# Low parts of the mixed and normed inputs all on VectorE, first products of the mixing all on ScalarE

## Chip, cores and metric

The kernel runs on one core of a Trainium2 chip. The metric is the device time of one execution in microseconds (us). The engines are TensorE (PE; its weight loads are PEld), VectorE (DVE), ScalarE (ACT), GpSimd (POOL) and SyncE (SP). Each takes its own instructions in order; they wait for each other by semaphores.

## What is computed

The model is a trunk of two layers, each followed by a SwiGLU FFN, on 1024 tokens of width 1024 in float32. The first layer mixes by chunked gating and by pooling, the second is RWKV-7 time mixing with a recurrence over the tokens. The change touches how the inputs of the RWKV-7 layer are made:

```python
def rwkv7_time_mix(h, mu, w_r, w_k, w_v, ...):
    xx = jnp.pad(h, ((0, 0), (1, 0), (0, 0)))[:, :-1] - h
    xr, xw, xk, xv, xa, xg = [h + xx * mu[i] for i in range(6)]
    r = xr @ w_r
    wlog = -jax.nn.softplus(-(w0 + jnp.tanh(xw @ w1) @ w2)) - 0.5
    k = xk @ w_k
    v = xv @ w_v
    a = jax.nn.sigmoid(a0 + (xa @ a1) @ a2)
    g = jax.nn.sigmoid(xg @ g1) @ g2
    ...
    y = wkv7_scan(rh, decay, kh, vh, -kk, kk * ah)
    ...
    return (y * g) @ w_o

def swiglu(hn, w_gate, w_up, w_down):
    return (jax.nn.silu(hn @ w_gate) * (hn @ w_up)) @ w_down
```

Here `h` is the normed input of the layer. A mixed input such as `xg` is, for every channel, `h[t] * (1 - mu) + h[t-1] * mu`.

## The kernel before

Tokens are worked in two halves of 512, channels in eight tiles of 128 (`KT` = 8). A float32 operand of a matmul is split into a high part that PE takes in its fast float32 format and a low part, the rest; a product is then three matmuls (`mm3`, L344 to L346: high by high, high by low, low by high). The split of a tile is a copy to the high part on ACT (L145) and a subtraction for the low part (L146), on DVE unless another engine is named. Weights come by DMA from ACT's queue (L115) into a ring of three `raw` tiles and are split in the same way into `whi` and `wlo`; some small weights go through `stack` (L151 on ACT, L153 on DVE), among them `w2` and `a2`, shown as `w` and `a` in the profile.

The order of the program: the first layer for both halves, then for each half the projections and the recurrence of the RWKV-7 layer, with parts of the FFNs of either half worked beside them so that PE has dense work. `beside` (L694) runs such a part of an FFN (and for the second half the output projection of the first) and, between its matmuls, the steps of `side` (in `project_gate`): the split of the normed input in eight steps (`split_steps`, 128 x 513 a tile, one token more than a half), then `mix_steps` for the inputs of `g`, `r` and `k`. That is one stage for each half. `project` then makes `k`, `r` and the decay for one pair of heads after another, mixes the input of `v` by a fourth call of `mix_steps`, and multiplies it. `recur` (the recurrence) comes next, again with FFN work beside it.

`mix_steps` makes for each of the eight tiles: a first product `mix = hn * (1 - mu)` (L882 on DVE or L886 on ACT, by the table `MIX_ENG`: even tiles ACT, odd tiles DVE), a second product with a sum (L887 on DVE, the shifted input times `mu`, added in place), a high part on ACT (L891) and a low part (L875, by the table `LOW_ENG`: even tiles DVE, odd tiles POOL). The low part of a tile is written in the code after the high part of the next one. The `mix` tiles have two buffers, so the first product of a tile waits until the low part of the tile two before it has been made. For `g`, `k` and `v` the parts are called `xhi` and `xlo`, for `r` and for the normed input `ahi` and `alo`.

Other work on POOL near the change: the scaling after a sigmoid (`sigm`, L775), the square root by a power (`rsqrt`, L349; in `project` on `rn`, the norms of the keys, which PE then spreads by L1037), `kkn` (L1051), and the clearing of tiles for the inversion (L1111).

Instructions are not issued in the order of the code: a scheduler with a timeline model of the engines sets the order on each of them, so that an edit in one place can move instructions elsewhere.

Of the kernel before, what the change touches and what calls it, by code (L numbers as in the profile page):

```python
# [9 lines left out]
F32 = mybir.dt.float32  # L10
F32R = mybir.dt.float32r
AF = mybir.ActivationFunctionType
ALU = mybir.AluOpType
# [9 lines left out]
GN_EPS = 64e-5  # L23
DEC = math.exp(-0.5)
WINS = (2, 4, 8, 16)

MIX_ENG, LOW_ENG = "adadadad", "dpdpdpdp"


RATIO, AHEAD, INV, FINE = 3.0, 450, 5, 1  # L30
# [8 lines left out]
def tile_trunk(  # L39
# [8 lines left out]
    act, dve, pool, pe, sp = nc.scalar, nc.vector, nc.gpsimd, nc.tensor, nc.sync  # L48
    x = x.flatten_outer_dims()
    out = out.flatten_outer_dims()  # L50
# [43 lines left out]
    omv = const.tile([P, P], F32, name="omv")  # L94

    def col(c):
        return vec[:, c : c + 1]
# [35 lines left out]
    def take(key):  # L133
        i = pos[0]
        assert plan[i][0] == key, (plan[i][0], key)
        pos[0] += 1
        split_at(i)
        load_at(i + 1)
        if i + 1 in raws:
            load_at(i + 2)  # L140
        split_at(i + 1)
        return ready.pop(i)

    def split(src, hi, lo, eng=None):
        act.activation(hi, src, AF.Copy)  # L145
        (eng or dve).tensor_tensor(out=lo, in0=src, in1=hi.bitcast(F32), op=ALU.subtract)  # L146

    def stack(los):

        def go(n, src, dst, _):  # L150
            act.activation(dst, src, AF.Copy)  # L151
            r = los[n]
            dve.tensor_tensor(out=dst[r], in0=src[r], in1=dst[r].bitcast(F32), op=ALU.subtract)  # L153

        return go
# [19 lines left out]
    def v3(t):  # L175
        return t.rearrange("p (k m) -> p k m", m=P)
# [79 lines left out]
    def groups_of(first):  # L256

        rest = list(range(first, 18))
        return [[f, f + 1] for f in range(0, first, 2)], [rest[i : i + 3] for i in range(0, len(rest), 3)], [18, 19], [20, 21]

    n0, n1, a, b = groups_of(BESIDE[0])
    G0B = n0, n1 + [a], [b]
    n0, n1, a, b = groups_of(BESIDE[1])
# [65 lines left out]
    def mmt():  # L329
        return pst("mm")  # L330
# [12 lines left out]
    def mm3(o, whi, wlo, xhi, xlo, first, last):  # L343
        pe.matmul(o, whi, xhi, start=first, stop=False)  # L344
        pe.matmul(o, whi, xlo, start=False, stop=False)  # L345
        pe.matmul(o, wlo, xhi, start=False, stop=last)  # L346
# [37 lines left out]
    def act_tiles(pool_, n=HT):  # L384
        return [pool_.tile([P, KT, n], F32R, tag=t, name=t) for t in ("ahi", "alo")]
# [113 lines left out]
    for h in range(2):  # L499
        ops = [mmt() for _ in range(4)]  # L500
        for kp in range(4):
# [4 lines left out]
            for kk in range(2):  # L506
                k = 2 * kp + kk
# [11 lines left out]
    for tt in range(8):  # L519
        dve.tensor_scalar(  # L520
            out=vt[tt], in0=vt[tt], scalar1=vss[:, tt : tt + 1], scalar2=None, op0=ALU.mult
# [46 lines left out]
    for m in ORD_Z:  # L568
# [4 lines left out]
        for h in range(2):  # L573
# [22 lines left out]
            if h == 0:  # L596
                dve.scalar_tensor_tensor(
                    out=s[:, 16 : 16 + win - 1], in0=s[:, 16 : 16 + win - 1], scalar=float(win),
                    in1=tcnt[:, 0 : win - 1], op0=ALU.mult, op1=ALU.mult,
                )  # L600
            dve.scalar_tensor_tensor(
                out=zq, in0=s[:, 16:], scalar=1.0 / win, in1=zp[:, 16:], op0=ALU.mult, op1=ALU.subtract,
# [13 lines left out]
    for h in range(2):  # L616
        hi, lo = act_tiles((xlp, actp)[h])
# [148 lines left out]
    def dense2(o, whi, wlo, xs, n=P, between=()):  # L766

        wh, wl = v3(whi), v3(wlo)
        for k in range(KT):
            if k < len(between):  # L770
                between[k]()
            mm3(o, wh[:, k, :n], wl[:, k, :n], xs[k][0], xs[k][1], k == 0, k == KT - 1)

    def sigm(dst, th):
        pool.tensor_scalar(out=dst, in0=th, scalar1=0.5, scalar2=0.5, op0=ALU.mult, op1=ALU.add)  # L775
# [14 lines left out]
    def project_norm(h, np_):  # L790

        hn1 = np_.tile([P, KT, 1 + HT], F32, name="hn1")
        if h == 0:
            pool.memset(hn1[:, :, 0:1], 0.0)
        else:
            pool.tensor_copy(hn1[:, :, 0:1], hlast)
        b = norm_scale(h)
        for k in range(KT):
            dve.scalar_tensor_tensor(
                out=hn1[:, k, 1:], in0=H[h][:, k, :], scalar=col(C_MIX + 8 + k), in1=b, op0=ALU.mult, op1=ALU.mult  # L800
            )
        if h == 0:
            pool.tensor_copy(hlast, hn1[:, :, HT : HT + 1])
        return hn1

    def project_gate(h, hn1, kp, xlp, ring):

        xlow = act_tiles(xlp, 1 + HT)
        keep = {}

        def tile_of(tag):
            keep[tag] = kp.tile([P, HT], F32R, tag=tag, name=tag)
            return keep[tag]

        def split_steps():
            for k in range(KT):  # L820
                split(hn1[:, k, :], xlow[0][:, k, :], xlow[1][:, k, :], pool if k % 2 else dve)
                yield

        def lowrank():

            ws = [take(("wa1", h, n)) for n in range(2)]
            o = mmt()
            for k in range(KT):
                for n, (wh, wl) in enumerate(ws):
                    sl = slice(1 - n, 1 - n + HT)  # L830
                    xh, xl = (x[:, k, sl] for x in xlow)
                    mm3(o, v3(wh)[:, k, :], v3(wl)[:, k, :], xh, xl, k == 0 and n == 0, k == KT - 1 and n == 1)
            t = nt.tile([P, HT], F32, tag="nsq", bufs=2, name="low")
            act.activation(t[0:64], o[0:64], AF.Tanh)
            act.activation(t[64:128], o[64:128], AF.Copy)
            lo = tile_of("twlo")
            for n, tag in enumerate(("tw", "ta")):
                hi = tile_of(tag)
                for r in rows:
                    act.activation(hi[r], t[rows[n]], AF.Copy)  # L840
                r = rows[n]
                dve.tensor_tensor(out=lo[r], in0=t[r], in1=hi[r].bitcast(F32), op=ALU.subtract)

        xs = []

        def gate():
            for nm, n in (("g1", P), ("g1b", 96)):
                wg = take((nm, h))
                o = mmt()
                dense2(o[:n], *wg, xs, n)  # L850
                t = nt.tile([P, HT], F32, tag="nsq", bufs=2, name="gt")
                act.activation(t[:n], o[:n], AF.Tanh, scale=0.5)
                sigm(t[:n], t[:n])
                if n == P:
                    split(t, tile_of("ghi"), tile_of("glo"))
                else:
                    stack([slice(64, 96)])(0, t[:n], tile_of("gst")[:n], None)

        def side():
            yield from split_steps()  # L860
            yield from mix_steps(hn1, 5, xs, ring_tiles(ring), kp)
            xr = [x.rearrange("p k t -> p (k t)")[:, : KT * HT].rearrange("p (k t) -> p k t", t=HT) for x in act_tiles(xlp, 1 + HT)]
            yield from mix_steps(hn1, 0, keep["xr"], lambda k: [x[:, k, :] for x in xr], kp)
            yield from mix_steps(hn1, 2, keep["xk"], ring_tiles(ring), kp)

        keep["xr"], keep["xk"] = [], []
        return (side(), lowrank, gate), keep

    def ring_tiles(ring):
        return lambda k: [ring.tile([P, HT], F32R, tag=tag, bufs=8, name=tag) for tag in ("xhi", "xlo")]  # L870

    def mix_steps(hn1, i, res, tiles, kp):

        def low(k, t, hi, lo):
            (pool if LOW_ENG[k] == "p" else dve).tensor_tensor(out=lo, in0=t, in1=hi.bitcast(F32), op=ALU.subtract)  # L875

        prev = None
        for k in range(KT):
            c = C_MU + 8 * i + k
            t = kp.tile([P, HT], F32, tag="mix", bufs=2, name="mix")  # L880
            if MIX_ENG[k] != "a":
                (dve if MIX_ENG[k] == "d" else pool).tensor_scalar(  # L882
                    out=t, in0=hn1[:, k, 1:], scalar1=omv[:, c : c + 1], scalar2=None, op0=ALU.mult
                )
            else:
                act.activation(t, hn1[:, k, 1:], AF.Identity, scale=omv[:, c : c + 1])  # L886
            dve.scalar_tensor_tensor(  # L887
                out=t, in0=hn1[:, k, 0:HT], scalar=col(c), in1=t, op0=ALU.mult, op1=ALU.add
            )
            hi, lo = tiles(k)  # L890
            act.activation(hi, t, AF.Copy)  # L891
            if prev is not None:
                low(*prev)
            prev = k, t, hi, lo
            if k == KT - 1:
                low(*prev)
            res.append((hi, lo))
            yield
# [236 lines left out]
    for b in range(2):  # L1135
        for c0, cmp in ((0, ALU.is_gt), (64, ALU.is_ge)):
            v = gm[rows[b], c0 : c0 + 64]
            pool.affine_select(
                out=v, in_=v, pattern=[[1, 64]], compare_op=cmp, fill=0.0, base=0, channel_multiplier=-1
# [354 lines left out]
    hn1 = project_norm(0, np_)  # L1494
# [43 lines left out]
    hn1 = project_norm(1, np_)  # L1538
# [85 lines left out]
```

## Time and profile before

| | us |
|---|---|
| median of three runs | 2528.8 |
| lowest and highest | 2524.71 and 2532.28 |
| the profiled execution, its own time | 2522.66 |
| its span in the profile | 2520.9 |

The span runs from the first to the last instruction of the profiled execution. The mean clock that PE was granted in it is 0.983 of full speed. How PE's pace, the waits and the other engines look in the stages of the mixing is read in the prediction. Rows of a group read as: line, engine, operation, output and inputs, shapes, count, then busy us and mean ns of one, then the idle time ahead of them and what ended it. Rows of a timeline begin with the start and the duration in us.

The 40 slices of the page (63 us each) show where the stages lie; POOL is busiest where inputs are mixed, in the slices 11 to 14 and 23 to 26:

```
DVE  5445634444865873555457855964654445434443
ACT  6233322222544432333234643433333224323223
POOL 0200000000323410111001222401211000100001
```

### The profile page before, as it was taken

The numbers are of one execution on the slowest core, as the hardware profiler recorded it, in microseconds if no ns is written. First come the engines' busy times: TensorE is split into PE (matmuls) and PEld (weight loads), VectorE is DVE, ScalarE is ACT, GpSimd is POOL, SyncE is SP. The second block draws the span as 40 slices with busy tenths as digits, with TensorE's granted clock in tenths as the row PEclk, the third lists the DMA queues.
The fourth block names the chain that finished last, engine by engine and source line by source line (L and its number), as shares of the span: only waits on it lengthen the run. The fifth ranks groups of instructions, "written<-read, shape, count | busy, mean of one in ns | idle before, by whom it ended". The sixth has DMA issues, their size and how long they took to land.

```text
span 2520.9 us, 37945 instructions
## 1 busy us (share of the span) xinstructions
PE 2432.2 (96%) x15735; PEld 1983.2 (79%) x15735; DVE 1401.8 (56%) x2118; ACT 890.7 (35%) x1335; POOL 299.8 (12%) x298
## 2 busy tenths in 40 slices
PE   8999999999989998999999989899999999999998
PEld 6888888888767786788877667787888878888887
DVE  5445634444865873555457855964654445434443
ACT  6233322222544432333234643433333224323223
POOL 0200000000323410111001222401211000100001
PEclk9999999999999998999999999999999999999999
DMA  5113433323255478433334355585653332423331
GB/s 175 48 59 92 142 109 116 101 92 112 88 156 134 123 204 203 136 113 102 112 118 138 111 179 133 132 230 159 167 150 110 100 107 77 150 88 119 94 92 59
DMA packets 434956, 310.69 MB, mean 123 GB/s; under 512 B 93216, under 2 KB 395424, under 8 KB 433760
## 3 DMA queue, kind: packets, MB, share of 16 engines
q10 hardware_dynamic: 297280, 210.53, 27.9%
q1 hardware_dynamic: 137504, 97.75, 13.7%
q8 instruction: 123, 2.02, 0.3%
q14 instruction: 49, 0.40, 0.0%
HBM read 254.68 MB, written 53.54 MB: 122 GB/s over the span
## 4 chain that ended last, share of the span: by engine, by line
PE 74%; DVE 13%; DMA 7%; issue 3%; ACT 2%; POOL 1%; SPq 0%; ACTq 0%; DVEq 0%; POOLq 0%
PE mm L344 21%; PE mm L345 21%; PE mm L346 20%; PE sm L1168 4%; DVE wlo L146 2%; DMA raw<-in_ffn_w_up_dram 2%; DVE it L1117 1%; DVE mix L887 1%; DVE xi L1122 1%; DMA iat<-at_d 1%; PE yp L1168 1%; DMA raw<-in_ffn_w_down_dram 1%; PE mm L510 1%; PE mm L511 1%; ACT whi L145 1%
## 5 line engine op out<-in xcount | busy, mean ns | idle before, releaser
L344 PE MATMUL mm<-ahi,whi 128*128 128x512 f32 x1952 | 766.9, 394 | 5.1 <-DVE h L423 4.0
L345 PE MATMUL mm<-alo,whi 128*128 128x512 f32 x1952 | 769.1, 394 | 1.6 <-DVE alo L146 1.6
L346 PE MATMUL mm<-ahi,wlo 128*128 128x512 f32 x1952 | 766.5, 393 | 2.6 <-DVE wlo L146 2.6
L145 ACT ACTIVATE whi<-raw 128x1024 fp32r<-128x1024 f32 x288 | 304.3, 1058 | 768.1 <-PE mm L345 608.5
L146 DVE TENSOR_TENSOR wlo<-raw,whi 128x1024 fp32r<-128x1024 f32 x288 | 362.0, 1257 | 309.8 <-ACT whi L145 301.5
L344 PEld LDWEIGHTS mm<-ahi,whi 128*128 128x128 f32 x1952 | 367.9, 189 | 87.2 <-issue 4.5
L346 PEld LDWEIGHTS mm<-ahi,wlo 128*128 128x128 f32 x1952 | 368.2, 189 | 82.3 <-DVE wlo L146 3.4
L345 PEld LDWEIGHTS mm<-alo,whi 128*128 128x128 f32 x1952 | 368.2, 189 | 82.1 <-issue 3.7
L345 PE MATMUL mm<-hidlo,wdhi 128*128 128x512 f32 x624 | 246.6, 395 | 1.3 <-DVE hidlo L672 1.2
L344 PE MATMUL mm<-hidhi,wdhi 128*128 128x512 f32 x624 | 239.8, 394 | 6.6 <-ACT hidhi L671 5.2
L346 PE MATMUL mm<-hidhi,wdlo 128*128 128x512 f32 x624 | 245.5, 393 | 0.0
L423 DVE TENSOR_TENSOR h<-h,mm 128x512 f32<-128x512 f32 x192 | 129.2, 684 | 149.9 <-PE mm L346 149.1
L145 ACT ACTIVATE wdhi<-raw 128x1024 fp32r<-128x1024 f32 x82 | 86.6, 1059 | 254.9 <-DMA raw<-in_ffn_w_down_dram 150.8
L146 DVE TENSOR_TENSOR wdlo<-raw,wdhi 128x1024 fp32r<-128x1024 f32 x82 | 100.4, 1225 | 111.3 <-ACT wdhi L145 105.5
L668 DVE TENSOR_TENSOR sg<-sg,mm 128x512 f32<-128x512 f32 x88 | 60.2, 685 | 165.3 <-PE mm L346 164.9
L344 PEld LDWEIGHTS mm<-hidhi,wdhi 128*128 128x128 f32 x624 | 117.2, 188 | 35.2 <-ACT hidhi L671 7.4
L345 PEld LDWEIGHTS mm<-hidlo,wdhi 128*128 128x128 f32 x624 | 118.2, 189 | 27.9 <-DVE hidlo L672 3.2
L346 PEld LDWEIGHTS mm<-hidhi,wdlo 128*128 128x128 f32 x624 | 118.2, 189 | 24.6 <-issue 0.2
L423 DVE TENSOR_TENSOR hA<-hA,mm 128x512 f32<-128x512 f32 x72 | 48.7, 685 | 77.0 <-PE mm L346 77.0
L349 POOL TENSOR_TENSOR nrs<-nrs,small 128x4 f32<-128x4 f32 x8 | 10.0, 1246 | 625.4 <-DVE nrs L371 625.4
L344 PE MATMUL mm<-xhi,whi 128*128 128x512 f32 (+1 forms) x160 | 66.0, 412 | 4.2 <-ACT k L925 4.2
L672 DVE TENSOR_TENSOR hidlo<-sg,hidhi 128x512 fp32r<-128x512 f32 x88 | 64.5, 733 | 3.8 <-ACT hidhi L671 3.7
(300 smaller groups left out, 2952.1 us busy)
## 6 DMA issues: line engine op xcount, KB each, us to landing
raw<-in_ffn_w_gate_dram ACTq DMA_DIRECT2D x88, 512.0 KB
raw<-in_ffn_w_up_dram ACTq DMA_DIRECT2D x88, 512.0 KB
raw<-in_ffn_w_down_dram ACTq DMA_DIRECT2D x88, 512.0 KB
raw<-in_ab_w_in_dram ACTq DMA_DIRECT2D x16, 512.0 KB
raw<-in_ab_w_out_dram ACTq DMA_DIRECT2D x16, 512.0 KB
raw<-in_rwkv_w_k_dram ACTq DMA_DIRECT2D x16, 512.0 KB
raw<-in_rwkv_w_r_dram ACTq DMA_DIRECT2D x16, 512.0 KB
ar_d<-ar SPq DMA_DIRECT2D x16, 512.0 KB
```

Source lines behind the costliest of these rows:

```text
L145: act.activation(hi, src, AF.Copy)
L146: (eng or dve).tensor_tensor(out=lo, in0=src, in1=hi.bitcast(F32), op=ALU.subtract)
L344: pe.matmul(o, whi, xhi, start=first, stop=False)
L345: pe.matmul(o, whi, xlo, start=False, stop=False)
L346: pe.matmul(o, wlo, xhi, start=False, stop=last)
L423: dve.tensor_tensor(out=H[h][:, m, :], in0=H[h][:, m, :], in1=o, op=ALU.add)
L510: pe.matmul(ops[j], xhi[:, k, sl], whi[:, kk], start=(k == 0), stop=False)
L511: pe.matmul(ops[j], xhi[:, k, sl], wlo[:, kk], start=False, stop=False)
L668: dve.tensor_tensor(out=s, in0=s, in1=o, op=ALU.mult)
L672: dve.tensor_tensor(out=lo, in0=s, in1=hi.bitcast(F32), op=ALU.subtract)
L887: dve.scalar_tensor_tensor(out=t, in0=hn1[:, k, 0:HT], scalar=col(c), in1=t, op0=ALU.mult, op1=ALU.add)
L1168: i = f(*args, **kw)
```

## The change

```diff
--- before.py
+++ after.py
@@ -23,8 +23,6 @@
 GN_EPS = 64e-5
 DEC = math.exp(-0.5)
 WINS = (2, 4, 8, 16)
-
-MIX_ENG, LOW_ENG = "adadadad", "dpdpdpdp"
 
 
 RATIO, AHEAD, INV, FINE = 3.0, 450, 5, 1
@@ -818,7 +816,7 @@
 
         def split_steps():
             for k in range(KT):
-                split(hn1[:, k, :], xlow[0][:, k, :], xlow[1][:, k, :], pool if k % 2 else dve)
+                split(hn1[:, k, :], xlow[0][:, k, :], xlow[1][:, k, :])
                 yield
 
         def lowrank():
@@ -872,18 +870,13 @@
     def mix_steps(hn1, i, res, tiles, kp):
 
         def low(k, t, hi, lo):
-            (pool if LOW_ENG[k] == "p" else dve).tensor_tensor(out=lo, in0=t, in1=hi.bitcast(F32), op=ALU.subtract)
+            dve.tensor_tensor(out=lo, in0=t, in1=hi.bitcast(F32), op=ALU.subtract)
 
         prev = None
         for k in range(KT):
             c = C_MU + 8 * i + k
             t = kp.tile([P, HT], F32, tag="mix", bufs=2, name="mix")
-            if MIX_ENG[k] != "a":
-                (dve if MIX_ENG[k] == "d" else pool).tensor_scalar(
-                    out=t, in0=hn1[:, k, 1:], scalar1=omv[:, c : c + 1], scalar2=None, op0=ALU.mult
-                )
-            else:
-                act.activation(t, hn1[:, k, 1:], AF.Identity, scale=omv[:, c : c + 1])
+            act.activation(t, hn1[:, k, 1:], AF.Identity, scale=omv[:, c : c + 1])
             dve.scalar_tensor_tensor(
                 out=t, in0=hn1[:, k, 0:HT], scalar=col(c), in1=t, op0=ALU.mult, op1=ALU.add
             )
```

`mix_steps` is called eight times and makes 64 mixed tiles. For the 32 odd ones the first product moves from DVE to ACT and the low part from POOL to DVE. The split of the normed input makes 16 tiles, of which eight low parts move from POOL to DVE. Nothing else in the code is changed; lines after the table move up by two, those after the loop of `mix_steps` by seven, so L887, L891 and L875 of before are L880, L884 and L873 of the change.

How the order on the engines comes out is shown at three places. The first is on DVE, in the mixing of the input of `g` for the first half; the numbers in the names tell the tiles apart (`mix_4559` is the third of the eight, `mix_4569` the fourth). Before:

```order
L882 TENSOR_SCALAR mix_4569<-hn1_4353,omv_74 128x512
L887 SCALAR_TENSOR_TENSOR mix_4559<-hn1_4353,vec_73,mix_4559 128x512
L887 SCALAR_TENSOR_TENSOR mix_4569<-hn1_4353,vec_73,mix_4569 128x512
L875 TENSOR_TENSOR xlo_4563<-mix_4559,xhi_4562 128x512
L887 SCALAR_TENSOR_TENSOR mix_4579<-hn1_4353,vec_73,mix_4579 128x512
L882 TENSOR_SCALAR mix_4589<-hn1_4353,omv_74 128x512
L887 SCALAR_TENSOR_TENSOR mix_4589<-hn1_4353,vec_73,mix_4589 128x512
L875 TENSOR_TENSOR xlo_4583<-mix_4579,xhi_4582 128x512
```

The same four tiles on DVE in the change:

```order
L880 SCALAR_TENSOR_TENSOR mix_4559<-hn1_4353,vec_73,mix_4559 128x512
L880 SCALAR_TENSOR_TENSOR mix_4569<-hn1_4353,vec_73,mix_4569 128x512
L873 TENSOR_TENSOR xlo_4563<-mix_4559,xhi_4562 128x512
L873 TENSOR_TENSOR xlo_4573<-mix_4569,xhi_4572 128x512
L880 SCALAR_TENSOR_TENSOR mix_4579<-hn1_4353,vec_73,mix_4579 128x512
L880 SCALAR_TENSOR_TENSOR mix_4589<-hn1_4353,vec_73,mix_4589 128x512
L873 TENSOR_TENSOR xlo_4583<-mix_4579,xhi_4582 128x512
L873 TENSOR_TENSOR xlo_4593<-mix_4589,xhi_4592 128x512
```

The two first products are gone and two low parts have come, and the tiles go in pairs; ahead of the second pair of sums stand on ACT the first products of `mix_4579` and `mix_4589`.

The second place is on DVE at the end of the same stage, where PE needs the weight `w2` for the first pair of heads in `project`; `mix_6561` and `mix_6567` are the first two tiles of the input of `v`. Before:

```order
L153 TENSOR_TENSOR whi_5189<-raw_5090,whi_5189 32x1024
L887 SCALAR_TENSOR_TENSOR mix_6561<-hn1_4353,vec_73,mix_6561 128x512
L882 TENSOR_SCALAR mix_6567<-hn1_4353,omv_74 128x512
L887 SCALAR_TENSOR_TENSOR mix_6567<-hn1_4353,vec_73,mix_6567 128x512
L153 TENSOR_TENSOR w2_5184<-raw_5186,w2_5184 64x1024
L153 TENSOR_TENSOR a2_5185<-raw_5192,a2_5185 64x1024
```

In the change:

```order
L151 TENSOR_TENSOR whi_5189<-raw_5090,whi_5189 32x1024
L873 TENSOR_TENSOR xlo_5014<-mix_5010,xhi_5013 128x512
L873 TENSOR_TENSOR xlo_5021<-mix_5017,xhi_5020 128x512
L880 SCALAR_TENSOR_TENSOR mix_6561<-hn1_4353,vec_73,mix_6561 128x512
L151 TENSOR_TENSOR w2_5184<-raw_5186,w2_5184 64x1024
L151 TENSOR_TENSOR a2_5185<-raw_5192,a2_5185 64x1024
L880 SCALAR_TENSOR_TENSOR mix_6567<-hn1_4353,vec_73,mix_6567 128x512
```

Between the splits of `whi` and `w2` stand now two low parts of the input of `k` and one sum, where two sums and a product stood; the second sum comes behind both splits.

The third place is on POOL in the last pairs of heads of the first half, where the input of `v` is mixed. Before:

```order
L349 TENSOR_TENSOR rn_6283<-rn_6283,small_70 128x8
L875 TENSOR_TENSOR xlo_6571<-mix_6567,xhi_6570 128x512
L1048 TENSOR_SCALAR ar_6342<-kkn_6344 128x8
L875 TENSOR_TENSOR xlo_6585<-mix_6581,xhi_6584 128x512
L1051 TENSOR_TENSOR kkn_6344<-kkn_6344,av_6263 128x512
L775 TENSOR_SCALAR sg_6438<-sg_6438 128x512
L775 TENSOR_SCALAR av_6439<-av_6439 128x512
L875 TENSOR_TENSOR xlo_6599<-mix_6595,xhi_6598 128x512
L1017 COPY pct_1943<-epx_6448 128x8
L349 TENSOR_TENSOR rn_6459<-rn_6459,small_70 128x8
```

In the change:

```order
L347 TENSOR_TENSOR rn_6283<-rn_6283,small_70 128x8
L1041 TENSOR_SCALAR ar_6342<-kkn_6344 128x8
L1044 TENSOR_TENSOR kkn_6344<-kkn_6344,av_6263 128x512
L773 TENSOR_SCALAR sg_6438<-sg_6438 128x512
L773 TENSOR_SCALAR av_6439<-av_6439 128x512
L1010 COPY pct_1943<-epx_6448 128x8
L347 TENSOR_TENSOR rn_6459<-rn_6459,small_70 128x8
```

The low parts are gone from between the steps of the projection; the rest stands in the same order.

## The prediction

> **What bounds the kernel now.** The page comes first. TensorE (PE) is busy for 96% of the span and holds 74% of the chain that ended last; VectorE (DVE) holds 13%, ScalarE (ACT) 2% and GpSimd (POOL) 1%.
>
> ```profile
> PE 2432.2 (96%) x15735; PEld 1983.2 (79%) x15735; DVE 1401.8 (56%) x2118; ACT 890.7 (35%) x1335; POOL 299.8 (12%) x298
> PE 74%; DVE 13%; DMA 7%; issue 3%; ACT 2%; POOL 1%; SPq 0%; ACTq 0%; DVEq 0%; POOLq 0%
> ```
>
> A change that touches no matmul can therefore only win or lose idle time of PE, and only in the stages where it acts. There are four: the two stages in which the mixing runs beside dense work (once for each half of the tokens), and the two in which the v products are mixed. The busy times of PE, PE's loads, DVE, ACT and POOL in them, then PE's clock:
>
> ```profile
> 637.00:727.00 90.00, 78.30 (x334) 61.42 (x332) 84.91 (x106) 54.38 (x82) 30.08 (x26) 0.98 0.34 105
> 1357.00:1467.00 110.00, 96.27 (x400) 73.48 (x399) 98.70 (x129) 62.38 (x95) 33.70 (x26) 0.98 0.41 132
> 855.00:890.00 35.00, 32.00 (x184) 24.98 (x184) 32.62 (x53) 16.68 (x25) 18.70 (x13) 0.85 0.52 137
> 1598.00:1631.00 33.00, 26.45 (x199) 20.61 (x197) 31.11 (x48) 14.90 (x22) 17.53 (x13) 1.00 0.48 134
> ```
>
> DVE is the fullest engine in all four (84.91 of 90 us, 94%, in the first), while PE is idle for 11.7 us of the first and 13.7 us of the second. In these stages DVE sets the pace, although over the whole span it is busy 56%. The waits of PE say the same (us in total, times, longest). Around the first mixing stage:
>
> ```profile
> PE aux L999 <- DVE w L153: 4.6, 1, 4.6
> PE mm L344 <- ACT whi L145: 2.3, 1, 2.3
> PE mm L923 <- DVE whi L153: 2.1, 1, 2.1
> PE mm L344 <- DVE sg L668: 1.5, 1, 1.5
> ```
>
> Around the second:
>
> ```profile
> PE mm L344 <- DVE h L423: 4.0, 1, 4.0
> PE mm L346 <- DVE wlo L146: 2.6, 2, 2.1
> PE aux L999 <- DVE w L153: 1.9, 1, 1.9
> PE mm L345 <- DVE hidlo L672: 1.8, 1, 1.8
> ```
>
> And around each v mixing, the same row in both:
>
> ```profile
> PE aux L1037 <- POOL rn L349: 2.6, 1, 2.6
> ```
>
> Of the first group 8.2 us end on DVE (4.6 + 2.1 + 1.5) and 2.3 us on ACT; the four rows of the second make 10.3 us.
>
> **The change part by part.** Each of the 64 mixed tiles has a first product, a second product with the sum (L887), a high part on ACT (L891) and a low part (L875). For the odd tiles the product leaves DVE (L882) for ACT (L886), and the low part leaves POOL for DVE. Eight lows of the normed input leave POOL too. Durations (min/median/max, ns):
>
> ```profile
> L882 DVE TENSOR_SCALAR mix<-hn,omv x32: 469/475/1907, 643.0 to 1618.1; 128x512 f32<-128x512 f32 x32
> L886 ACT ACTIVATE mix<-hn,omv x32: 706/720/727, 639.1 to 1616.8; 128x512 f32<-128x512 f32 x32
> L875 POOL TENSOR_TENSOR xlo<-mix,xhi x24: 1273/1648/2742, 651.3 to 1626.4; 128x512 fp32r<-128x512 f32 x24
> L875 DVE TENSOR_TENSOR xlo<-mix,xhi x24: 677/678/919, 653.6 to 1628.7; 128x512 fp32r<-128x512 f32 x24
> L887 DVE SCALAR_TENSOR_TENSOR mix<-hn,vec,mix x64: 736/741/1835, 644.7 to 1622.6; 128x512 f32<-128x512 f32 x64
> L146 DVE TENSOR_TENSOR wlo<-raw,whi x288: 951/1225/2356, 13.5 to 2471.9; 128x1024 fp32r<-128x1024 f32 x143, 128x768 fp32r<-128x768 f32 x1
> ```
>
> *Work moved, one mixing stage beside dense work.* Three input sets of eight tiles: DVE loses 12 products, 12 x 0.475 = 5.7 us, and gains 12 lows, 12 x 0.678 = 8.1 us, and 4 lows of the normed input, 4 x 0.68 = 2.7 us. Counted by work alone DVE gets **5.1 us more** on the fullest engine. ACT gets 12 x 0.720 = 8.6 us, which takes it from 54.4 to 63 of 90 us.
>
> *The stretch that goes.* Against that stands what POOL's instructions do to DVE's. The same timeline on POOL, DVE and ACT, where POOL works on one low:
>
> ```profile
> 676.79 3.55 POOL L875 TENSOR_TENSOR alo<-mix,ahi 128x512 fp32r<-128x512 f32 x1 [5.00 <-issue]
> 679.11 1.52 DVE L882 TENSOR_SCALAR mix<-hn,omv 128x512 f32<-128x512 f32 x1
> 680.38 0.72 ACT L886 ACTIVATE mix<-hn,omv 128x512 f32<-128x512 f32 x1 [3.72 <-POOL alo L875]
> 681.13 0.75 DVE L887 SCALAR_TENSOR_TENSOR mix<-hn,vec,mix 128x512 f32<-128x512 f32 x1 [0.51 <-ACT mix L886]
> ```
>
> The product that takes 0.475 us alone takes 1.52 us and ends just after POOL does; POOL's own low takes 3.55 us where its shortest takes 1.27; and ACT stood 3.72 us before the next product, because the tile's buffer was free only when POOL was done, after which DVE stood 0.51 us. The groups of DVE in the first stage show how often that happens:
>
> ```profile
> L887 DVE SCALAR_TENSOR_TENSOR mix<-hn,vec,mix 128x512 f32<-128x512 f32 x26 | 23.5, 916 | 2.6 <-ACT mix L886 2.5
> L146 DVE TENSOR_TENSOR wlo<-raw,whi 128x1024 fp32r<-128x1024 f32 x11 | 15.7, 1432 | 0.3 <-ACT whi L145 0.3
> L882 DVE TENSOR_SCALAR mix<-hn,omv 128x512 f32<-128x512 f32 x13 | 9.3, 718 | 0.0
> L875 DVE TENSOR_TENSOR alo<-mix,ahi 128x512 fp32r<-128x512 f32 x4 | 4.9, 1228 | 0.0
> L1111 POOL MEMSET xi<- 128x2048 f32 x1 | 1.8, 1799 | 0.0
> ```
>
> Means above the medians: 26 x (916 - 741) = 4.6 us, 11 x (1432 - 1225) = 2.3, 13 x (718 - 475) = 3.2, 4 x (1228 - 678) = 2.2; together 12.3 us. The last row is POOL work at the stage's end that stays; a DVE instruction that meets it loses up to its 1.8 us, of which I leave 1.5, so **10.8 us go** with the change.
>
> The Trainium skill, SBUF — State Buffer, section "Who interferes with whom", says that GpSimd and a DVE instruction with two SBUF inputs (or in a two-port mode) lock the same port pair for a whole instruction and that the later one blocks. The direction agrees with the four rows; by the full lock 16 lows at the 1.27 us of the shortest could cost up to 20 us a stage, an estimate, where the groups show 10.8: often POOL is the one held up (its 3.55 us), and no engine needed that result soon. By the full 20 us the time would be that of the fourth rival, since PE cannot win more than it waits; the sum goes by the groups.
>
> The second stage:
>
> ```profile
> L887 DVE SCALAR_TENSOR_TENSOR mix<-hn,vec,mix 128x512 f32<-128x512 f32 x26 | 25.5, 989 | 0.1
> L146 DVE TENSOR_TENSOR wlo<-raw,whi 128x1024 fp32r<-128x1024 f32 x13 | 16.9, 1310 | 0.2 <-ACT whi L145 0.2
> L882 DVE TENSOR_SCALAR mix<-hn,omv 128x512 f32<-128x512 f32 x13 | 7.3, 558 | 0.0
> ```
>
> By the same medians 6.4 + 1.1 + 1.1 = 8.6 us; with the 2.2 us of the lows taken over from the first stage it is 10.8 us again.
>
> *The wait that is added.* DVE's own product needed no other engine. Now all 24 come from ACT, and there are two buffers for the mixed tile, so the order goes in pairs: two L887, two lows, then two products on ACT, each of which needs a buffer that a low has just freed. If nothing stands between, the next L887 starts when low (0.68), product (0.72) have run one behind the other, while DVE fills 0.68 of that with the second low: about 0.3 us per pair lost in semaphores and ACT's longer instruction, 12 pairs, 3.6 us. Where DVE has weight splits or sums of the residual to do between, it is nothing. Behind a waiting product on ACT stand weight highs (L145) and the DMA issues of the next weights. The nearest row before is the 2.5 us that L887 waited for L886. I take 1.8 us, with 0 and 5.7 us (all that the moved products save) as ends.
>
> Sum for a mixing stage on DVE: -10.8 + 5.1 + 1.8 = **-3.9 us**. PE waits there on DVE for 8.2 and 10.3 us, more than that, so I let PE have all of it: **-4 us, twice**. The largest piece is at the end of the stage: ahead of the split of `w2` (wait of 4.6 us) DVE now has one L887 and two lows, before it had two L887 and a product beside POOL's L1111.
>
> *The v mixing.* Here POOL also works for the projections, in order:
>
> ```profile
> 865.92 1.29 POOL L875 TENSOR_TENSOR xlo<-mix,xhi 128x512 fp32r<-128x512 f32 x1
> 867.17 1.29 POOL L1051 TENSOR_TENSOR kkn<-kkn,av 128x512 f32<-128x512 f32 x1
> 867.25 1.50 DVE L882 TENSOR_SCALAR mix<-hn,omv 128x512 f32<-128x512 f32 x1 [1.40 <-POOL xlo L875]
> 875.91 2.04 POOL L349 TENSOR_TENSOR rn<-rn,small 128x8 f32<-128x8 f32 x1 [0.97 <-DVE rn L1026]
> ```
>
> The low holds up `kkn`, the product on DVE waits 1.40 us for it and takes 1.50 us; the path goes on over `rn` to PE, which waits 2.6 us (the row of waits above). Removed: 1.4 us of wait and, for four lows in the proportion of the first stage (10.8 us for 16), 2.7 us of stretch, of which the product shown has 1.0; added: 4 x (0.678 - 0.475) = 0.8 us, and 0.6 us for two of the four pairs of products. Net -2.7 us on DVE, of which PE can get its 2.6: **-2.5 us, twice**.
>
> Together 2 x 4 + 2 x 2.5 = **13 us**. The profiled execution, 2522.66 us with a span of 2520.9, would become about 2509.7; it lies 6.1 us below the median of the runs, so the median of 2528.8 becomes 2515.8, say **2515.5**.
>
> **The rivals.** (1) *PE gets only part.* The wait is taken over by what was second: at `w2` the next weights, in other places ACT's weight highs (2.3 us in the rows of waits). For it: that row stands second in its group. Against it: the longest waits, 4.6 and 4.0 us, end on DVE. If PE gets half, the sum is 6.5 us and the time 2522. (2) *ACT becomes the late engine (slower).* If the order puts a weight high (mean 1058 ns, the row below) between a high part and the next product in every pair, DVE waits for it 12 times a stage, 12.7 us, besides the 3.6; a stage then comes to -10.8 + 5.1 + 3.6 + 12.7 = +10.6 us. Twice that less the 5 us of the v mixing is +16: 2545.
>
> ```profile
> L145 ACT ACTIVATE whi<-raw 128x1024 fp32r<-128x1024 f32 x288 | 304.3, 1058 | 768.1 <-PE mm L345 608.5
> ```
>
> It decides from the point where DVE waits for L886 by more than 5.7 us a stage; before, that row is 2.5 us. Against it: ACT is at 70% of the stage and its idle time goes mostly to DVE and PE, not to loads.
>
> (3) *The order elsewhere.* The scheduler also moves matmuls in the recursion of both halves. The waits there:
>
> ```profile
> PE sm L1168 <- DVE gt L1215: 6.7, 5, 2.6
> PE sm L1168 <- DVE gt L1215: 4.1, 1, 4.1
> ```
>
> are those of the first and the second half. If both halves pay the larger or the gaps turn up at new places, I count 6 us lost: 2522; if the first half loses its own, 6 us more are won: 2509. (4) *All the stretch is won*: nothing waits for ACT and the ends of the dense work close up too. Stage: -5.7 each, v mixing -3.3 each, 18 us; and PE's clock, 0.85 in the first v stage where the second has 1.00, comes back when the gap goes: 0.15 x 35 = 5 us more. 2505.5. (5) *The stretch is not POOL's.* Then only the moved work counts: 2 x 5.1 + 2 x 0.8 = +12, 2540. Against it: the rows in which both engines end together.
>
> **How the numbers follow.** Two measurements of this kernel can be told apart by about 0.3%, 7.6 us. Chances: the forecast 0.50, all of the stretch 0.13, PE gets part 0.18, the order elsewhere 0.08, ACT late 0.08, the stretch not POOL's 0.03. Faster by over 0.3% are the first two and half of the third rival's good side: 0.66. Within 0.3%: 0.23. Slower: 0.11. The range takes in the forecast with the ends of the added wait (0 to 5.7 us a stage: 2512 to 2523), the part gain, the order elsewhere and most of the larger gain: 2502 to 2531.
>
> **What would show it.** In the mixing stages the mean of L887 falls from 916 and 989 to about 745 ns, wlo from 1432 to about 1230, and DVE's busy time by 5 to 6 us a stage; POOL's share goes from 12% to about 9%. The waits for `w` L153, `sg`, `hidlo` and `h` shrink by some 4 us a stage; `rn` falls from 2.6 to near 0. Right in mechanism but wrong in size: L887 waits on L886 for more than 1.8 us a stage. Wrong: L887 still near 900 ns without POOL; or PE's waits pass to ACT `whi`; or the recursions (940 to 1215 and 1680 to 1960 us before) change length by more than 3 us.

## The result, and the profile after

The changed kernel takes **2510.5 us** (median of 4 runs, 2509.5 to 2513.2) against 2526.8 us for the kernel before, run beside it: ratio 0.9938, 95% interval 0.9922 to 0.9954, or 11.6 to 19.7 us less. The profiled execution took 2509.54 us, with a span of 2507.4. The forecast was 2515.5, from 13 us gained.

The page of the changed kernel, its busy times and its chain:

```profile
PE 2432.2 (97%) x15735; PEld 1985.9 (79%) x15735; DVE 1382.5 (55%) x2126; ACT 909.8 (36%) x1367; POOL 240.0 (10%) x258
PE 79%; DVE 8%; DMA 7%; ACT 2%; issue 2%; SPq 1%; POOL 1%; ACTq 0%; POOLq 0%; DVEq 0%
```

PE's busy time is to the tenth what it was, and DVE, with eight instructions more, works 19.3 us less. On the chain PE rose from 74 to 79% of the span and DVE fell from 13 to 8%. The windows of the first and the second mixing stage (PE, PE's loads, DVE, ACT, POOL; ends set to the same matmuls as before):

```profile
636.50:718.40 81.90, 77.75 (x334) 61.58 (x332) 77.18 (x108) 60.75 (x93) 5.26 (x10) 0.99 0.36 110
1344.20:1446.00 101.80, 94.85 (x401) 73.24 (x401) 91.88 (x132) 70.98 (x109) 6.93 (x10) 0.99 0.45 143
```

The first is 8.1 us shorter than the 90 us of before, with DVE at 77.2 us in place of 84.9; the second is 8.2 us shorter, with DVE at 91.9 us in place of 98.7. PE is now the fullest engine of both. The groups of DVE in the first stage:

```profile
L880 DVE SCALAR_TENSOR_TENSOR mix<-hn,vec,mix 128x512 f32<-128x512 f32 x25 | 18.9, 770 | 0.8 <-ACT mix L879 0.6
L144 DVE TENSOR_TENSOR wlo<-raw,whi 128x1024 fp32r<-128x1024 f32 x11 | 13.4, 1220 | 2.4 <-ACT whi L143 2.4
L873 DVE TENSOR_TENSOR xlo<-mix,xhi 128x512 fp32r<-128x512 f32 x16 | 10.7, 687 | 0.1
```

The second product has a mean of 770 ns (916 before), the weights' lows of 1220 (1432). The wait of the second product for ACT's first product, which the prediction let grow by 1.8 us, fell from 2.5 to 0.6 us. PE's waits around the first mixing stage, and then around the first v mixing with the start of the recurrence:

```profile
PE aux L992 <- DVE w L151: 2.7, 1, 2.7
PE mm L916 <- DVE whi L151: 0.8, 1, 0.8
PE mm L344 <- DVE wlo L144: 0.4, 1, 0.4
PE mm L342 <- ACT hidhi L669: 0.3, 1, 0.3
...
PE sm L1163 <- DMA bk<-bk_d: 4.3, 1, 4.3
...
PE aux L1030 <- POOL rn L347: 0.3, 1, 0.3
```

Of `w` (4.6 us), `whi` from ACT (2.3), `whi` L153 (2.1) and `sg` (1.5) are left 2.7 and 0.8 us, and `rn` went from 2.6 to 0.3 us. All rows of PE's waits together fell from 13.8 to 4.2 us around the first mixing stage and from 16.1 to 9.0 us around the second. One row grew: the wait for the DMA that brings `bk`, the first input of the recurrence. Before, it was

```profile
PE sm L1170 <- DMA bk<-bk_d: 1.9, 1, 1.9
```

in the first half and none in the second, where it is 3.5 us now.

Where the time went is best read from PE's matmuls, since there are 15735 of them in both traces: by how much later (+) or earlier (-) than in the first profile of before does the matmul of the same number run, and by how much does that grow in each part? The columns end at the matmuls that ran at 760, 926, 1340, 1480, 1668 and 1975 us before; "recurrence" includes the FFN beside it. All rows are profiles, in us; those below the first come from the runs told further down.

| profile | mixing 1 | projections, v mixing 1 | recurrence 1 | mixing 2 | projections, v mixing 2 | recurrence 2 |
|---|---|---|---|---|---|---|
| changed | -10.1 | -4.0 | +1.8 | -8.2 | -4.9 | +11.5 |
| changed, second profile (e6) | -10.9 | -4.1 | -2.1 | -8.1 | -3.9 | +14.8 |
| before, second profile (e5) | +2.3 | +1.9 | -2.0 | +1.8 | -1.7 | +8.7 |
| e1, lows alone | -8.2 | +0.1 | -1.8 | -3.6 | -3.4 | +11.9 |
| e2, products alone | -0.9 | +0.1 | -1.5 | -0.5 | -1.5 | +10.9 |
| e3, POOL kept busy | +1.9 | -4.1 | -1.7 | +0.6 | -3.9 | +20.6 |
| e4, v mixing as before | -6.5 | -0.1 | -4.0 | -8.7 | -2.2 | +6.7 |
| e7, before, wide descriptors | +1.7 | +1.5 | -3.1 | +2.5 | -1.4 | +2.4 |
| e8, changed, wide descriptors | -10.0 | -3.9 | +1.6 | -8.1 | -3.8 | +12.7 |
| e9, changed, third profile | -10.9 | -3.8 | -5.4 | -8.1 | -4.5 | +13.8 |
| e10, xi_d from POOL | -9.9 | -4.0 | -10.6 | -9.0 | -5.5 | +10.8 |
| e11, before, xi_d from POOL | +2.3 | +1.9 | -8.7 | +1.7 | -2.0 | +10.1 |
| e12, e10 again | -10.2 | -3.8 | -10.4 | -8.8 | -5.3 | +7.1 |

The four stages of the mixing gained 27.2 us in the first row, twice the forecast, and the second recurrence gave 11.5 us back. So there are two questions: which part of the change brings the 27 us, and what takes the rest away.

### The profile page after: what moved, and what is told of

Same layout as the page of the kernel before. It is cut to its first block, busy times and chain, and to the rows that moved or that the text cites. A ratio compares the mean times of both kernels' runs of the same rounds, so it can differ in the third digit from the quotient of the medians.

```text
span 2507.4 us, 37920 instructions
## 1 busy us (share of the span) xinstructions
PE 2432.2 (97%) x15735; PEld 1985.9 (79%) x15735; DVE 1382.5 (55%) x2126; ACT 909.8 (36%) x1367; POOL 240.0 (10%) x258
## 4 chain that ended last, share of the span: by engine, by line
PE 79%; DVE 8%; DMA 7%; ACT 2%; issue 2%; SPq 1%; POOL 1%; ACTq 0%; POOLq 0%; DVEq 0%
PE mm L343 22%; PE mm L342 22%; PE mm L344 22%; PE sm L1161 4%; DVE wlo L144 2%; DMA raw<-in_ffn_w_up_dram 1%; PE yp L1161 1%; DMA lnw<-in_rwkv_ln_w_dram 1%; DMA iat<-at_d 1%; DVE xi L1115 1%; DMA raw<-in_ffn_w_down_dram 1%; DVE it L1110 1%; DMA raw<-n_d 1%; DMA ar<-ar_d 1%; DVE alo L144 1%
```

## Experiments on the gain

**e1: the lows alone.**

```diff
-MIX_ENG, LOW_ENG = "adadadad", "dpdpdpdp"
+MIX_ENG, LOW_ENG = "adadadad", "dddddddd"
...
-                split(hn1[:, k, :], xlow[0][:, k, :], xlow[1][:, k, :], pool if k % 2 else dve)
+                split(hn1[:, k, :], xlow[0][:, k, :], xlow[1][:, k, :])
```

> Only the low parts move from POOL to DVE (odd mixed tiles and odd tiles of the normed input); odd first products stay on DVE. Measured for the whole change, by how much earlier the same matmul runs than before: first mixing stage 10.1 us, first v mixing 4.0, second mixing stage 8.3, second v mixing 4.8, and 11.6 given back in the second recurrence. Theory A (POOL's instructions stretch those of DVE) and theory B (a tile's buffer is held until POOL's slow low is done): the means of the second product fall to about 745 ns, DVE keeps 5.7 us of products a stage, each mixing stage gains 4 to 6 us, the time is 2514 to 2520. Theory C (what counts is the product taken off DVE): the stages gain 2 us or less, 2524 or more.

Measured: 2520.0 us, ratio 0.9976 [0.9961, 0.9990], 6 us less than before. The groups of DVE in its first mixing stage:

```profile
L887 DVE SCALAR_TENSOR_TENSOR mix<-hn,vec,mix 128x512 f32<-128x512 f32 x25 | 18.3, 747 | 0.2
L146 DVE TENSOR_TENSOR wlo<-raw,whi 128x1024 fp32r<-128x1024 f32 x11 | 13.3, 1218 | 0.0
L882 DVE TENSOR_SCALAR mix<-hn,omv 128x512 f32<-128x512 f32 x12 | 5.8, 480 | 0.1
```

With no low on POOL each of them is back at its median. The first mixing stage gains 8.2 us, the second 3.6, where 4 to 6 was expected of each: DVE still carries the 5.7 us of products there.

**e2: the products alone.**

```diff
-MIX_ENG, LOW_ENG = "adadadad", "dpdpdpdp"
+MIX_ENG, LOW_ENG = "aaaaaaaa", "dpdpdpdp"
```

> Only the odd first products move from DVE to ACT; the odd low parts stay on POOL. Theories A and B: the second product still has a mean near 900 ns in the mixing stages, each stage gains 2 to 4 us (DVE has 5.7 us less work, but waits more for products whose buffers POOL holds), the v mixings gain 1 us or less, the time is 2519 to 2525. Theory C: 8 us and more a stage, 2512 or less.

Measured: 2525.8 us, ratio 0.9999 [0.9983, 1.0014], no change. That was half a miss: A and B let the stages gain 2 to 4 us, and they gained 0.9 and 0.5. The mean of the second product is 877 ns in the second stage, near the 900 expected, and more in the first. DVE and ACT in the first:

```profile
L887 DVE SCALAR_TENSOR_TENSOR mix<-hn,vec,mix 128x512 f32<-128x512 f32 x25 | 25.3, 1020 | 4.2 <-ACT mix L886 4.2
L886 ACT ACTIVATE mix<-hn,omv 128x512 f32<-128x512 f32 x26 | 18.4, 717 | 7.5 <-POOL alo L875 3.4 <-DVE xlo L875 2.3 <-POOL xlo L875 1.7
```

While the lows are on POOL, taking 12 products off DVE brings next to nothing: the second product is stretched more (1020 ns against 916), and it waits 4.2 us for ACT, which waits 5.1 us for POOL's lows to free the buffer. This is the price at which the forecast's added wait would have hurt. The lows alone (-6 us) and the products alone (0) do not add up to the change (-16 us): the products pay only once the lows have left POOL.

**e3: POOL kept busy.** The whole change, and POOL makes a subtraction that nothing reads for each odd tile of the two mixing stages (the split of the normed input has the same line).

```diff
             if prev is not None:
                 low(*prev)
...
+            if k % 2 and i != 3:
+                pool.tensor_tensor(out=dum[0], in0=hn1[:, k, 1:], in1=hi.bitcast(F32), op=ALU.subtract)
```

> The whole change, and for each odd tile of the two mixing stages (not of the v mixings) POOL makes one more subtraction of the same shape, of the normed input and the high part, into a tile that nothing reads: 16 a stage, contention without a buffer of the mixed tile behind it. Theory A: the second product is back at 880 ns and more, DVE's weight lows near 1400 ns, the mixing stages lose 5 us and more each against the change, and the time is 2517 to 2524. Theory B: DVE's instructions may be stretched but the stages keep 7 us and more of their gains, 2514 or less.

Measured: 2535.5 us, ratio 1.0042 [1.0025, 1.0060]; slower than before, and some 26 us slower than the change (1.0042 / 0.9938). The groups of DVE and of POOL in its second mixing stage:

```profile
L886 DVE SCALAR_TENSOR_TENSOR mix<-hn,vec,mix 128x512 f32<-128x512 f32 x24 | 22.2, 936 | 0.0
L144 DVE TENSOR_TENSOR wlo<-raw,whi 128x1024 fp32r<-128x1024 f32 x15 | 19.5, 1306 | 6.7 <-ACT whi L143 6.7
...
L897 POOL TENSOR_TENSOR dum<-hn,xhi 128x512 f32<-128x512 f32 x8 | 15.0, 1874 | 39.0 <-ACT xhi L890 39.0
```

The second product is back at 936 ns (758 in the change), and at 878 in the first stage (770), although no instruction of the trace waits for these subtractions. Both mixing stages lose all their gain (+1.9 and +0.6 us in the table), while the v mixings, which have no such instruction, keep theirs (-4.1 and -3.9 us). Contention (theory A) is shown; held buffers (theory B) are not needed for it, though e2 shows that they exist. The time is above the 2517 to 2524 expected: the two stages account for 20.8 us against the first profile of the change, and the second recurrence, where the edit adds nothing, for 9.1 more (+20.6 against +11.5), whose cause stays open. The Trainium skill, SBUF — State Buffer, section "Who interferes with whom", says that a DVE instruction with two SBUF inputs contends with a GpSimd instruction that reads SBUF; the 936 ns agree in kind.

**e4: the v mixing as before.**

```diff
-            dve.tensor_tensor(out=lo, in0=t, in1=hi.bitcast(F32), op=ALU.subtract)
+            (pool if i == 3 and k % 2 else dve).tensor_tensor(out=lo, in0=t, in1=hi.bitcast(F32), op=ALU.subtract)
...
-            act.activation(t, hn1[:, k, 1:], AF.Identity, scale=omv[:, c : c + 1])
+            if i == 3 and k % 2:
+                dve.tensor_scalar(
+                    out=t, in0=hn1[:, k, 1:], scalar1=omv[:, c : c + 1], scalar2=None, op0=ALU.mult
+                )
+            else:
+                act.activation(t, hn1[:, k, 1:], AF.Identity, scale=omv[:, c : c + 1])
```

> The change without the v mixing, whose odd products stay on DVE and odd lows on POOL. If what the v mixings win (4.0 and 4.8 us) reaches the end: 2519. Theory D (the start of each recurrence waits for DMAs, which do not come earlier when PE does): most of it is given back there anyway, PE's wait for bk falls from 4.3 and 3.5 us to about 2 and 0.5, and the time is 2511 to 2514.

Measured: 2512.8 us, ratio 0.9953 [0.9937, 0.9969]. The columns of the v mixing lose 3.9 and 2.7 us against the change, and the time only about 4 us (0.9953 against 0.9938, intervals that overlap). Its waits at the starts of the two recurrences:

```profile
PE sm L1168 <- DMA bk<-bk_d: 3.4, 1, 3.4
...
PE sm L1168 <- DMA bk<-bk_d: 2.3, 1, 2.3
```

They are 0.9 and 1.2 us shorter than in the change (4.3 and 3.5). If the earlier v matmuls are the reason, about a third of what the v mixing wins is given back at once; theory D had foreseen more.

## Experiments on what is given back

**e5 and e6: a second profile of each kernel, unchanged.**

> The kernel before, unchanged: a second profile of it. From the last v matmul of the second half to the first matmul of the recurrence (109 dense matmuls lie between, 24.5 us of work) it took 24.7 us, and to the 390th matmul 58.0 us; in every other recurrence profiled so far 26.6 to 29.5 and 61.7 to 66.0 us. If that was a matter of one execution, this look shows 61 us or more at the 390th; if the order or the timing of that kernel brings it about, again 57 to 59.

> The changed kernel, unchanged: a second profile. If the second recurrence's loss of 11.6 us belongs to it, it is there again within 3 us (66 us to the 390th matmul); if it is a matter of one execution, it differs by more.

Measured: before 2533.55 us and 64.1 us to the 390th matmul of the second recurrence; changed 2508.95 us and 63.5 us (66.0 in its first profile). So the 58.0 us of the first profile were a matter of that execution. Of the 11.5 us in the table's first row a good part is therefore the reference: the second profile of before has +8.7 in the same column. The mean of the two profiles of the change (+13.2) stands 8.8 us above the mean of the two of before (+4.4), and the third profile of the change (e9, +13.8) agrees. About half of the 8.8 is idle time of PE (13.8 and 12.6 us in the column against 5.2 and 12.1). The other half is the same matmuls taking longer (304.7 and 309.2 us against 301.7 and 303.4), with a granted clock of 0.98 and 0.97 against 0.99 and 0.98.

**e7 and e8: wider descriptors for the weight stream** beside mixing and recurrence, on both kernels. The rows read are those of another matrix, of as many bytes, so the products are not the model's.

```diff
-        if kind == "g":
+        if kind in ("g", "u") and h != l:
+            push((kind, l, h, f), rowblk(ffn_w_down[l], f * P))
+        elif kind == "g":
             push(("g", l, h, f), colblk(ffn_w_gate[l], f * P))
```

> The kernel before, with the gate and up weights of the two FFNs that run beside mixing and recurrence read as whole rows of another matrix, of the same number of bytes (wrong numbers): descriptors of 4 KB in place of 512 B. Theory D (the DMA stream bounds the start of the recurrences): the first matmul of both recurrences comes 24.5 to 25.5 us after the last v matmul, and the time falls by 10 us or more. Theory E (the order and the engines' own chain): no change at the 390th matmul, 2523 or more.

> The same edit on the changed kernel. Theory D: nothing is given back at the start of the recurrences, 58 us and less to the 390th matmul in both, and the distance to the kernel before with the same edit is 20 us or more (the four stages won 27). Theory E: the distance stays near 14 us.

Measured: 2520.9 us for the kernel before, ratio 0.9989 [0.9973, 1.0005], and 2509.2 us for the changed one, ratio 0.9936 [0.9913, 0.9960]. Nothing moved beyond the intervals, and the first matmul of the recurrence still came 26.3 and 28.0 us (e7) and 28.5 and 28.1 us (e8) after the last v matmul. Theory D falls as far as the width of the weights' descriptors goes; a lighter stream by fewer bytes was not tried. The distance between the two, 11.7 us, is near the 14 of theory E.

**e9 and e10: the order on SP's queue.** In the traces the load of `bk` is issued 15.1 to 16.6 us after the end of the last v matmul in the two profiles of before, and 17.2 to 18.3 us after it in those of the change: between the first profiles v came 14.5 and 25.9 us earlier, the load only 12.2 and 23.4. SP's timeline in the changed kernel, whose last v matmul ends at 1643.4:

```profile
1657.90 1.12 SPq L1119 DMA_DIRECT2D xi_d<-xi  x2
1659.12 1.80 SPq L1176 DMA_DIRECT2D ar<-ar_d  x1
1660.97 2.41 SPq L1178 DMA_DIRECT2D bk<-bk_d  x1
```

The first row is what holds it. The store of `xi_d` waits for the inversion, a chain of 62 small dependent instructions on DVE, and the loads stand behind it on SP. The waits of SP in the same stretch:

```profile
SPq L1119 <- DVE xi L1117: 9.0, 1, 9.0
```

The store waited 9.0 us in the first profile of before too, but there the chain ended 11.3 us after the last v matmul of the second half, and here 14.5. The chain takes 33 to 35 us in all profiles; what is later in the change is its start, since its first instruction waits longer for the load of its input `iat`. In the second half of before, then of the change:

```profile
DVE it L1117 <- DMA iat<-at_d: 2.8, 1, 2.8
...
DVE it L1110 <- DMA iat<-at_d: 5.6, 1, 5.6
```

That v comes earlier is not needed for this. In e2 the last v matmuls come only 1.2 and 4.7 us earlier than before, and yet PE waits 4.6 and 4.8 us for `bk`.

The edit takes only that store off SP; nothing else of the change is touched:

```diff
-            sp.dma_start(
+            (pool if p0 else sp).dma_start(
                 xi_d[h][q, p0 : p0 + 4].rearrange("p r c i a j -> (p r c) (i a j)"), xf[q * 64 : q * 64 + 64]
             )
```

> The changed kernel, unchanged, timed beside the next one: 2509 to 2513; the first matmul of the recurrences 28 to 29.5 us after the last v matmul, in both halves.

> The changed kernel; the stores of the second inversion's result (xi_d) are issued from POOL's queue, not SP's, so that the loads of ar and bk for the recurrence no longer stand on SP behind a store that waits for the chain of the inversion on DVE. Theory F (that chain, through SP's order, is what is late next when the v matmuls come earlier): bk is issued less than 10 us after the last v matmul instead of 17 to 18, the first matmul of the recurrence comes at 24.5 to 25.5 us, PE's waits for bk (4.3 and 3.5 us) go, and the time falls by 3 to 8 us against the changed kernel. Theory D (the DMA stream itself is late): bk is issued earlier and lands no earlier, the first matmul stays at 28 us.

Measured: the changed kernel again 2512.1 us, ratio 0.9941 [0.9923, 0.9959]; with the edit **2494.3 us**, ratio 0.9868 [0.9844, 0.9892]. SP's timeline there, whose last v matmul ends at 1630.2, and the first matmul of the recurrence:

```profile
1636.16 0.35 SPq L1176 DMA_DIRECT2D ar<-ar_d  x1
1636.76 0.40 SPq L1178 DMA_DIRECT2D bk<-bk_d  x1
...
1655.32 0.32 PE L1163 MATMUL sm<-ar,bk 64*64 64x128 f32 x1
```

`bk` is issued 6.5 us after the last v matmul, and the recurrence begins 25.1 us after it, which is the work that stands between (28.8 us in e9). PE no longer waits for `bk` in either half. The time fell by about 18 us, more than the 3 to 8 expected; the two waits account for 7.8 us. Another part is the clock: the mean that PE was granted over the four executions of each is 0.983 in e9 and 0.987 in e10, and 0.4% of 2494 us is about 10 us, an estimate. Why the clock is higher no run here shows.

**e11 and e12: the same edit on the kernel before, and e10 again beside it.**

> The kernel before, with the stores of the second inversion issued from POOL's queue as in e10. If the changed kernel lost at the start of the recurrences what only this order took from it (theory F), the edit is worth less here, since the first matmul of the recurrence came 24.7 to 28 us after the last v matmul already: 3 to 6 us, 2520 to 2524, and the distance between this kernel and e10 is larger than the 15.7 us between before and after, 20 us and more. If the edit helps both alike, 2510 to 2516.

> e10 again, beside e11 on the same chip: 2487 to 2500, and 20 us and more below e11 by theory F.

Measured: before with the edit 2522.6 us, ratio 0.9989 [0.9975, 1.0003]; the change with the edit **2493.0 us**, ratio 0.9873 [0.9855, 0.9891]. The edit is worth at most 0.25% on the kernel before and about 0.7% on the changed one, and the distance between the two grows from 16 to 29.6 us, about what the four stages win, as theory F said.

The store is only a part of that. On the pages of its three profiles (the first, e6, e9) the changed kernel has PE busy for 2432.1 us on average, and idle (the span less the busy time) for 73.2. In e10 and e12 it is busy for 2424.2 and idle for 68.8. So 4.4 us of the difference are idle time, and 7.9 us are the same 15735 matmuls in less time. The idle time falls by less than the 7.8 us of the two waits, since others took their place: soon after the start of the second recurrence of e10 PE waits 5.9 us for `gt` from DVE. The granted clock has a mean of 0.987 in e12 as in e10 and of 0.982 in e11, so that about 13 us of the 29.6 lie in the clock (an estimate from these means and 2500 us), as much as the distance grew. Between the kernel before (0.982) and the change (0.983) the clock hardly differs: their 16 us do not come from it.

What is shown is that PE's waits for `bk` end when the store leaves SP. That the store held back the rest of what the change loses is not: the column of the second recurrence stays at +10.8 and +7.1 us, and e11, with the same edit, stands there at +10.1. How waits, clock and the order that the scheduler then finds depend on each other was not separated: the edit moves matmuls in both recurrences, and e11 wins 6.7 us in the first of them over the second profile of before and loses 1.4 in the second.

## Why the prediction was right, and where its terms were not

The time, the sign and the range came out. That the sum came so near is luck: two errors cancel, since the stages won twice what was forecast and about the excess was lost behind them.

- *What bounds the kernel*: held. DVE set the pace of the mixing stages; PE's waits on it there are what went. That only idle time of PE can change held for the change too: PE is busy for 2432.2 us in both first profiles.
- *The stretch of 10.8 us a stage that goes*: held (e1, e3). In the first stage DVE's busy time fell by 7.7 us and in the second by 6.8, the moved work included; -10.8 and +5.1 had made 5.7, so the stretch was some 2 and 1 us larger.
- *The added wait of 1.8 us a stage*: failed, in sign for the first stage. The wait fell from 2.5 to 0.6 us there, and in the second stage DVE is idle for 0.1 us ahead of the second product, before and after. ACT waits 7.3 us for its buffers in the first stage (8.8 before) and 5.2 in the second (2.5 before), but issues the pair early enough. e2 shows the case that was feared, with the lows still on POOL: 4.2 us.
- *"PE waits there on DVE for more than that, so I let PE have all of it: -4 us, twice"*: this is the term that failed in size; it measured 10.1 and 8.2 us. With the figures above DVE's sum is -7.7 - 1.9 = -9.6 us in the first stage and -6.8 in the second. So PE got all of it, as said, and 0.5 and 1.4 us more: it was DVE's sum of -3.9 that was too small. The excess may lie in PE's waits that end on ACT (`whi` 2.3 us in the first stage), which went too; that they were late through DVE is not shown. The first rival, that PE gets half, was the wrong way round.
- *v mixing, -2.5 us twice*: 4.0 and 4.9 us. `rn` behaved as said (2.6 to 0.3 us). The rest is not explained, and the reference itself moves by 1.9 and 1.7 us here (e5).
- *Nothing is lost behind the stages*: failed, and the text's own sign of being wrong came, a recurrence that changes by more than 3 us. The text asked what is late next and looked for it inside the stages. Part of it is the load of `bk`, behind a store that waits for another chain on DVE: 7.8 us of waits in both halves, where the two profiles of before have 1.9 and 4.3. Another part is a lower granted clock in the second recurrence, and the rest stays open. The third rival (order elsewhere, about 6 us) had the right place and nearly the right price, at a chance of 0.08, but named the matmuls' order as its mechanism; whether that has a share is open.
- *ACT late, and stretch not POOL's*: neither came. e3 excludes the last.

With these terms the first pair of profiles reads: 27.2 us won in the stages, 13.3 given back in the two recurrences, 13.5 left between the spans. By the means of two profiles of each it is 29.3 won, 9.7 given back and 19.2 left; the medians of the executions say 16.

## What to carry to other kernels

When POOL and the engine that sets the pace both read SBUF, count the stretch of the latter's instructions (mean against median by group) before counting work: here 5.1 us more work on the fullest engine made its stages 8 to 10 us shorter. Two halves of such a move may each be worth little or nothing alone, when one frees the buffers that the other waits for. And when a stage becomes shorter, look at the first transfer of the next one and at what stands ahead of it in its queue: here one store, moved to an idle queue, ended 7.8 us of waits, and the kernel became 18 us faster. Before all of such a gain is put down to the edit, compare PE's busy time for the same matmuls and the granted clock: about 10 of these 18 us lie there.

## What was not expected of the hardware

Single executions of one kernel differ by more than their medians suggest, and in one place: the second recurrence of the unchanged kernel took 58.0 and 64.1 us to its 390th matmul in two profiles with the same order of matmuls. A difference of 6 us there cannot be read from one pair of traces. The granted clock differs as well: 0.984 to 0.990 in the four executions of e10, whose times are 2487.4 to 2500.1 us.
